# Last eight modulation rows beside the first group's quads, and a column order for the first three down products

## The chip, the cores and the metric

One core of a Trainium2 chip runs the whole program. The metric is device time in microseconds. Before the change three runs gave 2177.98, 2178.56 and 2180.01 us, median 2178.56 us.

## The reference

One decoder layer over 2048 tokens of width 1024, in float32. The modulation vector `mod` has 6 x 1024 values; its last 1024, `gate2`, scale only the result of the feed-forward part.

```python
def reference(x, c, positions, w_ada, b_ada, ...):
    mod = silu(c) @ w_ada + b_ada
    shift1, scale1, gate1, shift2, scale2, gate2 = split(mod, 6)
    h = modulate(rmsnorm(x, norm1_w), shift1, scale1)
    x = x + gate1 * hybrid_mixer(h, ...)      # attention heads and SSD heads
    h = modulate(rmsnorm(x, norm2_w), shift2, scale2)
    x = x + gate2 * swiglu(h, w_gate_up, w_down)   # (silu(g) * u) @ w_down
    return rmsnorm(x, final_norm_w)
```

## The kernel before

**Tiling.** Tokens are cut into four blocks of 512. A value is kept as [128 channels, 512 tokens]. Each float32 product is made of three fast matmuls: an operand is split into a rounded part (ScalarE, a copy) and a rest (VectorE, a subtraction), and hi x hi, hi x lo and lo x hi are added in one bank of PSUM. There are four rotating banks `d` (`dense()`) and four side banks.

**Stages.** First the input projections, attention and SSD of the blocks; then the feed-forward part in two groups of two blocks. The feed-forward products are of the Strassen kind: seven products take the place of eight. A *quad* (L1055 on, 22 per group) makes four weight tiles' worth of the gate/up part from seven products of 12 matmuls (lines 1050 to 1052), each with weights loaded into `raw` (5 buffers) and split into `w` (6 buffers). Its token operands are named b11, t1, b21, t2, t3, b22, t4. `quads` yields seven times per quad; `beside` hands every yield to `tick`, which moves side work on: attention and SSD of later blocks, and the modulation rows while `ada_rest` holds them.

**Modulation rows.** One row gives 128 values of `mod`. `ada_later` loads the row's two halves [128, 512] of `w_ada` into two buffers `aw` (L202) and reduces each against the silu row `csil` on VectorE (L208). `rest_of_ada` goes through rows 16 to 23, 32 to 39, 24 to 31 and 40 to 47, three ticks a row. Row 40 to 47 are `gate2`. They come last, while the second block's output projection and the last block's projections run.

**Down products.** `pairs.stage` makes one of seven down products per group, with 11 token tiles (index k) and four output columns c. `steps_of` cuts a product into 12 steps: a column c with a chunk of k (0 to 3, 4 to 7, 8 to 10). A step loads and splits its weight tile (L1174, L1177, L1178) and issues 12 or 9 matmuls (L1182). Columns go in pairs: c 0 and 1 through all three chunks, then c 2 and 3. After a column's last chunk `done` takes its bank: a copy into `t` for b11 (L1228); for b21 and t4 a residual block `t` is loaded (L1197), the bank is added to it (L1213) and it is stored. b11 and t4 start new banks, b21 goes on in those of b11.

The token tiles come from DRAM (`tokens_of`): a load (L1162), a ScalarE copy (L1163), a VectorE subtraction (L1164). They share 11 buffers `a`, one product's worth, so a token tile of the next product can only be loaded when the last matmul on its buffer is over. For the first three products of the first group the caller asks for four tiles after the ninth step, four after the tenth, and the last three after the twelfth. Beside them run `last_operands`, the operands of the second group (lines 914 to 932 and 1028 to 1041), on VectorE, ScalarE, GpSimd and the DMA queue.

**Order.** The program is written down in this order; a scheduler then sets each engine's order by a simulated timeline, except that PE keeps the written order up to the end of the last block's projections. `behind(engine)` keeps an instruction from going ahead of the one written just before it on that engine. Each engine works its list in order, SP's list of DMA issues too: an issue that waits holds up those behind it.

## Time and profile before

| what | value |
|---|---|
| three runs, median | 2178.56 us |
| profiled execution, its time | 2179.79 us |
| profiled execution, its span | 2177.7 us |
| mean granted TensorE clock | 0.997 |
| ACT busy, share of the span | 47% |
| POOL busy, share of the span | 25% |
| DMA moved | 466.76 MB, mean 214 GB/s |

The span is the time from the first to the last instruction of the profiled execution; 2.1 us lie around it. PE is TensorE's matmuls, PEld its weight loads, DVE is VectorE, ACT ScalarE, POOL GpSimd, SP the engine that issues the DMAs. In the rows that stand in the prediction a name such as `a<-act_t` reads "writes a, reads act_t", `L1182` is a line of the kernel, and "x12" a count.

### The profile page before, as it was taken

How to read it: one execution, taken by the hardware profiler on the slowest of the kernel's cores; microseconds unless marked ns; L12 is line 12 of the kernel's file. 1: busy time of each engine (PE TensorE's matmuls, PEld its weight loads, DVE VectorE, ACT ScalarE, POOL GpSimd, SP SyncE). 2: the span in 40 equal slices, each digit the busy share in tenths (PEclk: the TensorE clock that was granted, in tenths of full speed). 3: DMA queues.
4: the chain of work that ended last, by engine and by line, in shares of the span. 5: the costliest groups of instructions: out<-in, count | busy, mean ns of one | idle time of the engine just before them, and what ended most of it. 6: DMA issues, size and time to landing. Idle time of an engine off the chain costs nothing.

```text
span 2177.7 us, 33314 instructions
## 1 busy us (share of the span) xinstructions
PE 2139.7 (98%) x10984; PEld 1764.9 (81%) x10984; DVE 1651.1 (76%) x3195; ACT 1016.5 (47%) x2137; POOL 553.5 (25%) x658
## 2 busy tenths in 40 slices
PE   8989999999999999999999999999999999999998
PEld 6889898879778777788888878788888888888887
DVE  6987857885778866798897678777877765886576
ACT  3675735653557454433344445433333334554441
POOL 0223433322112211243441212333333331210011
PEclk9999999999999999999999999999999999999999
DMA  7798978797998332333335778645555536778553
GB/s 269 237 341 297 353 260 312 255 342 238 360 357 313 109 97 92 121 109 124 115 94 178 248 244 293 216 155 187 166 167 179 168 112 232 239 266 278 184 161 105
DMA packets 287708, 466.76 MB, mean 214 GB/s; under 512 B 27440, under 2 KB 97072, under 8 KB 287536
## 3 DMA queue, kind: packets, MB, share of 16 engines
q1 hardware_dynamic: 286960, 464.13, 63.3%
q8 instruction: 86, 1.41, 0.3%
q14 instruction: 86, 0.70, 0.1%
q10 hardware_dynamic: 576, 0.52, 0.1%
HBM read 329.73 MB, written 134.81 MB: 213 GB/s over the span
## 4 chain that ended last, share of the span: by engine, by line
PE 79%; DVE 8%; DMA 5%; ACT 3%; issue 2%; POOL 1%; SPq 0%; DVEq 0%; ACTq 0%; POOLq 0%
PE d L1182 17%; PE d L1052 9%; PE d L1051 9%; PE d L1050 9%; PE d L286 4%; PE d L287 4%; PE d L288 4%; DMA aw<-in_wada_dram 1%; PE d L1323 1%; PE am L1050 1%; PE am L1052 1%; PE am L1051 1%; PE am L706 1%; PE sm L1052 1%; PE sm L1051 1%
## 5 line engine op out<-in xcount | busy, mean ns | idle before, releaser
L1182 PE MATMUL d<-a,w 128*128 128x512 f32 x1716 | 403.5, 396 | 2.2 <-DVE a L1164 2.2
L1182 PEld LDWEIGHTS d<-a,w 128*128 128x128 f32 x1716 | 323.2, 189 | 79.6 <-DVE a L1164 2.9
L1052 PE MATMUL d<-b,w 128*128 128x512 f32 x924 | 366.9, 399 | 0.6 <-DVE w L898 0.6
L1051 PE MATMUL d<-b,w 128*128 128x512 f32 x924 | 366.6, 397 | 0.7 <-DVE b L932 0.5
L1050 PE MATMUL d<-b,w 128*128 128x512 f32 x924 | 363.2, 397 | 0.0
L897 ACT ACTIVATE w<-s 128x512 fp32r<-128x512 f32 x176 | 111.0, 631 | 237.2 <-PE d L1052 148.2
L1051 PEld LDWEIGHTS d<-b,w 128*128 128x128 f32 x924 | 174.2, 189 | 41.7 <-DVE b L932 1.5
L1052 PEld LDWEIGHTS d<-b,w 128*128 128x128 f32 x924 | 173.8, 188 | 40.4 <-DVE w L898 1.0
L1050 PEld LDWEIGHTS d<-b,w 128*128 128x128 f32 x924 | 174.2, 189 | 38.0
L286 PE MATMUL d<-w,hl 128*128 128x256 f32 (+1 forms) x592 | 171.9, 290 | 2.7 <-DVE s L511 2.7
L287 PE MATMUL d<-w,hl 128*128 128x256 f32 (+1 forms) x592 | 166.9, 282 | 0.0
L288 PE MATMUL d<-w,hl 128*128 128x256 f32 (+1 forms) x592 | 166.8, 282 | 0.0
L1178 DVE TENSOR_TENSOR w<-raw,w 128x512 fp32r<-128x512 f32 x156 | 114.0, 739 | 43.3 <-ACT w L1177 43.0
L1104 POOL TENSOR_TENSOR t<-t 128x512 f32<-128x512 f32 x44 | 75.5, 1717 | 277.0 <-DVE t L1103 126.1
L1164 DVE TENSOR_TENSOR a<-a 128x512 fp32r<-128x512 f32 x154 | 106.2, 704 | 46.1 <-ACT a L1163 45.3
L898 DVE TENSOR_TENSOR w<-s,w 128x512 fp32r<-128x512 f32 x176 | 131.1, 746 | 6.3 <-ACT w L897 5.4
L1163 ACT ACTIVATE a<-a 128x512 fp32r<-128x512 f32 x154 | 96.1, 629 | 85.1 <-DMA a<-act_t 50.1
L296 POOL TENSOR_TENSOR acc<-acc,t 128x512 f32<-128x512 f32 x35 | 51.8, 1481 | 325.7 <-ACT t L295 312.1
L286 PE MATMUL d<-hl,w 128*128 128x512 f32 x320 | 131.6, 411 | 0.0
L288 PE MATMUL d<-hl,w 128*128 128x512 f32 x320 | 126.1, 394 | 0.0
L1177 ACT ACTIVATE w<-raw 128x512 fp32r<-128x512 f32 x156 | 90.6, 587 | 75.8 <-PE d L1182 44.3
L287 PE MATMUL d<-hl,w 128*128 128x512 f32 x320 | 125.7, 393 | 0.0
(426 smaller groups left out, 4802.6 us busy)
## 6 DMA issues: line engine op xcount, KB each, us to landing
raw<-in_wgu_dram SPq DMA_DIRECT2D x176, 256.0 KB, 3.0
act_t<-t SPq DMA_DIRECT2D x88, 256.0 KB, 2.9
a<-act_t SPq DMA_DIRECT2D x88, 256.0 KB, 4.5
act_b<-t SPq DMA_DIRECT2D x66, 256.0 KB, 2.0
a<-act_b SPq DMA_DIRECT2D x66, 256.0 KB, 4.2
aw<-in_wada_dram SPq DMA_DIRECT2D x64, 256.0 KB, 5.1
w<-w_x SPq DMA_DIRECT2D x32, 512.0 KB, 5.5
raw<-wd_s SPq DMA_DIRECT2D x64, 256.0 KB, 3.2
```

Source lines behind the costliest of these rows:

```text
L286: nc.tensor.matmul(out, ahi, bhi, start=first, stop=False)
L287: nc.tensor.matmul(out, ahi, blo, start=False, stop=False)
L288: mm3.last = nc.tensor.matmul(out, alo, bhi, start=False, stop=last)
L897: nc.scalar.activation(hi, x, AF.Copy)
L898: eng.tensor_tensor(lo, x, hi.bitcast(F32), ALU.subtract)
L1050: nc.tensor.matmul(out, ahi, bhi, start=first and k == 0, stop=False, skip_group_check=True)
L1051: nc.tensor.matmul(out, ahi, blo, start=False, stop=False, skip_group_check=True)
L1052: mm3.last = nc.tensor.matmul(out, alo, bhi, start=False, stop=k == 3, skip_group_check=True)
L1163: nc.scalar.activation(hi, raw, AF.Copy)
L1164: nc.vector.tensor_tensor(lo, raw, hi.bitcast(F32), ALU.subtract)
L1178: nc.vector.tensor_tensor(w[1], raw, w[0].bitcast(F32), ALU.subtract)
L1182: mm3.last = nc.tensor.matmul(ps, w[x][:, ws], act[k][y], start=new and k == 0 and x + y == 0, stop=k == KP - 1 and x == 1, skip_group_che ...
```

## The change

Two edits. The first takes rows 40 to 47 out of `rest_of_ada`, stores the silu row in DRAM (`csil_d`), and makes the eight rows later, beside the first group's quads, from step 12 on: first the left halves of all eight rows, then the right halves, each through the one buffer `acc` of `sums()`, with half of the silu row at a time in a small pool that takes the place of a pool closed by then. The second gives `steps_of` a column order for the first three products: all four columns of a chunk of k before the next chunk, and a call for one token tile of the next product after each step from the fifth on.

```diff
-    def steps_of(act, src, banks, new, done):
-        for c, (lo, hi) in ((c + e, chunk) for c in (0, 2) for chunk in CHUNKS for e in range(2)):
+    def steps_of(act, src, banks, new, done, across):
+        order = [(c + e, chunk) for c in (0, 2) for chunk in CHUNKS for e in range(2)]
+        if across:
+            order = [(c, chunk) for chunk in CHUNKS for c in range(4)]
+        for c, (lo, hi) in order:
...
-            return steps_of(act, of, self.banks, name not in ("b21", "b22"), done)
+            return steps_of(act, of, self.banks, name not in ("b21", "b22"), done, not self.pool)
...
     def rest_of_ada():
-        for i in (*range(16, 24), *range(32, 40), *range(24, 32), *range(40, 48)):
+        for i in (*range(16, 24), *range(32, 40), *range(24, 32)):
             yield from ada_later(i)
...
+        with behind(mybir.EngineType.SP):
+            nc.sync.dma_start(csil_d, csil)
+    def gates_of_ada(pool):
+        parts = small([P, 8], "part", 1, pool=pool)
+        for half in range(2):
+            hs = slice(half * T, (half + 1) * T)
+            c = big("cs", 1, pool=pool)
+            with behind(mybir.EngineType.SP):
+                nc.sync.dma_start(c, csil_d[:, hs])
+            for j in range(8):
+                i = 40 + j
+                with behind(mybir.EngineType.SP):
+                    w = sums()
+                    nc.sync.dma_start(w, wada[i, :, hs])
+                for _ in range(2):
+                    yield
+                src, dst = (parts[:, j:j + 1], mod[:, i:i + 1]) if half else (b_ada[:, i:i + 1], parts[:, j:j + 1])
+                with behind(mybir.EngineType.DVE):
+                    nc.vector.tensor_tensor_reduce(w, w, c, 0.5, src, ALU.mult, ALU.add, dst)
+                yield
         nc.vector.tensor_scalar(gate2, gate2, 0.5, None, ALU.mult)
...
-    for _ in beside(main, lambda i: RATIO_UP if i >= 6 else 0):
+    ada_rest.clear()
+    gating = ExitStack()
+    rest = gates_of_ada(gating.enter_context(tc.tile_pool(name="gates", bufs=1, side="right")))
+    for i in beside(main, lambda i: RATIO_UP if i >= 6 else 0):
+        if i == 12:
+            ada_rest.append(rest)
         if not sides:
             break
     finish(sides[-1] if sides else None)
+    drain(rest)
+    ada_rest.clear()
+    gating.close()
...
-                if after and i in (8, 9):
-                    for _ in range(4):
-                        next(coming, None)
+                if after and i > 3:
+                    next(coming, None)
```

Where the change moves instructions, first PE at the start of the third product, t4. `d_...` is a column's bank, `a_...` a token tile, `w_...` a weight tile. Before, 14787 to 14799 are k 0 to 3, 14820 on k 4 and up, and 14902, 14920, 15014 are columns 0, 1, 2:

```order
L1182 MATMUL d_14902<-a_14799,w_14905 128x512 x2
L1182 MATMUL d_14920<-a_14787,w_14923 128x512 x2
L1182 MATMUL d_14920<-a_14791,w_14923 128x512 x3
L1182 MATMUL d_14920<-a_14795,w_14923 128x512 x3
L1182 MATMUL d_14920<-a_14799,w_14923 128x512 x3
L1182 MATMUL d_14902<-a_14820,w_14946 128x512
L1182 MATMUL d_14920<-a_14820,w_14963 128x512
L1182 MATMUL d_14902<-a_14820,w_14946 128x512 x2
L1182 MATMUL d_14902<-a_14824,w_14946 128x512
L1182 MATMUL d_14920<-a_14820,w_14963 128x512 x2
```

The same place now (k 0 to 3 are 14714 to 14777, k 4 is 14805; columns 14905, 14923, 14947, 14965):

```order
L1185 MATMUL d_14923<-a_14756,w_14926 128x512 x3
L1185 MATMUL d_14923<-a_14777,w_14926 128x512 x3
L1185 MATMUL d_14905<-a_14805,w_14985 128x512
L1185 MATMUL d_14947<-a_14714,w_14950 128x512 x3
L1185 MATMUL d_14947<-a_14735,w_14950 128x512 x3
L1185 MATMUL d_14947<-a_14756,w_14950 128x512 x3
L1185 MATMUL d_14947<-a_14777,w_14950 128x512 x3
L1185 MATMUL d_14965<-a_14714,w_14968 128x512 x3
L1185 MATMUL d_14965<-a_14735,w_14968 128x512 x3
L1185 MATMUL d_14965<-a_14756,w_14968 128x512 x3
L1185 MATMUL d_14965<-a_14777,w_14968 128x512 x3
L1185 MATMUL d_14905<-a_14805,w_14985 128x512 x2
```

Before, k 4 was wanted after 24 matmuls of the product; now 24 more on k 0 to 3 stand ahead of it, but for one hi x hi matmul of k 4, which stands where it was.

Second, DVE where the second product ends and the third begins. L1164 makes the rest of a token tile of t4, L1213 takes a bank of b21, L1178 is a weight tile, the others are second-group operands. Before, from the third bank of b21:

```order
L1036 TENSOR_TENSOR t<-t 128x512
L1213 SCALAR_TENSOR_TENSOR t<-d,mod,t 128x512
L932 TENSOR_TENSOR b<-t,b 128x512
L1178 TENSOR_TENSOR w<-raw,w 128x384
L1039 SCALAR_TENSOR_TENSOR t<-t,mod 128x512
L1213 SCALAR_TENSOR_TENSOR t<-d,mod,t 128x512
L1164 TENSOR_TENSOR a<-a 128x512
L1178 TENSOR_TENSOR w<-raw,w 128x384
L1164 TENSOR_TENSOR a<-a 128x512
```

The same place now, where L1178 is called L1181 and L1213 is L1216; the first L1164 rows are k 0 to 3 of t4, and the L1216 is the first bank of b21:

```order
L1164 TENSOR_TENSOR a<-a 128x512 x2
L1041 SCALAR_TENSOR_TENSOR t<-t,mod 128x512
L1181 TENSOR_TENSOR w<-raw,w 128x384
L1164 TENSOR_TENSOR a<-a 128x512
L932 TENSOR_TENSOR b<-t,b 128x512
L1164 TENSOR_TENSOR a<-a 128x512
L1181 TENSOR_TENSOR w<-raw,w 128x512
L921 SCALAR_TENSOR_TENSOR t<-t,scl_146,at 128x512
L1181 TENSOR_TENSOR w<-raw,w 128x512
L927 SCALAR_TENSOR_TENSOR b<-t,mod,b 128x512
L1216 SCALAR_TENSOR_TENSOR t<-d,mod,t 128x512
L1164 TENSOR_TENSOR a<-a 128x512
```

So k 0 to 3 now stand ahead of all four banks of b21, and k 4 (the last row) behind the first bank; before, k 4 stood behind the fourth.

Third, SP in the first group's quads. L903 loads quad weights, L1098 stores quad results, L1499 loads half of the silu row and L1504 half a modulation row into `acc`. Now:

```order
L1098 DMA act_t_219<-t 128x512
L1499 DMA cs<-csil_d 128x512
L1504 DMA acc<-in_wada_dram 128x512
L903 DMA raw<-in_wgu_dram 128x512
L1504 DMA acc<-in_wada_dram 128x512
L903 DMA raw<-in_wgu_dram 128x512
L1504 DMA acc<-in_wada_dram 128x512
L1098 DMA act_b_213<-t 128x512
```

The rows of L1499 and L1504 are new there, among the loads and stores of the quads. Each L1504 after the first waits until DVE has reduced the half row before it, since `acc` is one buffer; the weight loads and stores behind it wait too.

More of the change, by code (lines that the diff above doesn't have):

```diff
@@ L1484, in rest_of_ada @@
                 nc.vector.tensor_tensor(dsh, sh2[:, 4:8], sh2[:, 0:4], ALU.subtract)
+        with behind(mybir.EngineType.SP):
+            nc.sync.dma_start(csil_d, csil)
+    csil_d = dr.tile([P, D], F32, name="csil_d")
+    def gates_of_ada(pool):
[16 more added lines that the diff above has]
+                yield
         nc.vector.tensor_scalar(gate2, gate2, 0.5, None, ALU.mult)
```

## The prediction

> **What bounds the kernel now.** First the busy shares of the page, then its costliest group:
>
> ```profile
> PE 2139.7 (98%) x10984; PEld 1764.9 (81%) x10984; DVE 1651.1 (76%) x3195; ACT 1016.5 (47%) x2137; POOL 553.5 (25%) x658
> L1182 PE MATMUL d<-a,w 128*128 128x512 f32 x1716 | 403.5, 396 | 2.2 <-DVE a L1164 2.2
> ```
>
> PE is the bound. The down products (L1182) wait once, 2.2 us, for a token tile that VectorE splits. No edit here takes a matmul away, so all that can be won is time in which PE stands or runs slowly. The windows show how much there is of it. Columns: stretch, its length, then busy time (and instructions) of PE, PEld, DVE, ACT, POOL, then the granted clock, the DMA engines' share, GB/s:
>
> ```profile
> 100.00:150.00 50.00, 43.47 (x291) 38.21 (x289) 47.33 (x119) 41.27 (x96) 14.79 (x16) 1.00 0.93 329
> 574.00:645.00 71.00, 70.67 (x357) 55.11 (x356) 48.65 (x128) 36.27 (x88) 5.97 (x9) 1.00 0.98 343
> 686.00:716.00 30.00, 27.62 (x137) 20.83 (x137) 24.95 (x42) 22.12 (x49) 10.28 (x8) 0.94 0.69 246
> 735.00:910.00 175.00, 175.00 (x858) 136.31 (x857) 123.93 (x250) 89.77 (x216) 26.75 (x21) 1.00 0.32 100
> 1350.00:1400.00 50.00, 47.84 (x200) 38.20 (x199) 39.40 (x61) 27.13 (x48) 15.14 (x7) 0.97 0.82 284
> 1650.00:1700.00 50.00, 50.00 (x217) 40.59 (x217) 38.25 (x56) 17.03 (x30) 14.50 (x10) 1.00 0.60 193
> ```
>
> From 1650 to 1700 us PE does nothing but matmuls of 512 columns, 217 in 50 us, one per 0.230 us: full speed. From 1350 to 1400 us it does the same kind and gets through 200. The missing 17 are 17 x 0.230 = 3.9 us. The quads from 735 to 910 us lose nothing. In the first feed-forward steps, 686 to 716 us, PE is idle 2.4 us and the clock is below 1. The two low clocks, closer:
>
> ```profile
> 686.00:689.45 3.45, 2.48 (x18) 2.10 (x17) 2.09 (x8) 1.76 (x4) 1.04 (x1) 1.00 1.05 377
> 689.45:692.86 3.41, 3.30 (x10) 2.84 (x11) 1.94 (x8) 2.76 (x11) 0.00 (x0) 0.50 1.01 362
> 1364.90:1367.40 2.50, 0.36 (x2) 0.00 (x0) 2.50 (x4) 1.99 (x5) 0.65 (x1) 1.00 1.05 397
> 1368.70:1372.10 3.40, 3.40 (x10) 2.63 (x9) 3.40 (x7) 1.67 (x3) 2.27 (x1) 0.50 0.62 224
> ```
>
> Twice a wait of PE is followed by 3.4 us at half clock, in which half the work gets done: 1.7 us lost each time. So the loss around 1365 us is a wait of 2.15 us (row below) and 1.7 us of half clock, together 3.9 us: the same as the matmuls that are missing. That is the price of one late tile.
>
> **The second edit: the column order.** PE, then DVE, where the third product t4 begins:
>
> ```profile
> 1367.42 26.38 PE L1182 MATMUL d<-a,w 128*128 128x512 f32 x106 [2.15 <-DVE a L1164]
> ...
> 1362.59 0.74 DVE L1213 SCALAR_TENSOR_TENSOR t<-d,mod,t 128x512 f32<-128x512 f32 x1
> 1363.26 0.68 DVE L932 TENSOR_TENSOR b<-t,b 128x512 fp32r<-128x512 f32 x1
> 1363.86 0.55 DVE L1178 TENSOR_TENSOR w<-raw,w 128x384 fp32r<-128x384 f32 x1
> 1364.32 1.78 DVE L1039 SCALAR_TENSOR_TENSOR t<-t,mod 128x512 f32<-128x512 f32 x1
> 1366.03 0.74 DVE L1213 SCALAR_TENSOR_TENSOR t<-d,mod,t 128x512 f32<-128x512 f32 x1
> 1366.69 0.67 DVE L1164 TENSOR_TENSOR a<-a 128x512 fp32r<-128x512 f32 x1
> ```
>
> PE resumes when the L1164 of 1366.69 us ends: k 4, the fifth tile of t4. 106 matmuls follow of the product's 132, so 26 were done: the two steps on k 0 to 3 and a first pair on k 4. k 4 was late for two reasons. Its buffer came free only after the eighth step of b21, and it was wanted 24 x 0.230 = 5.5 us into t4. The edit moves both. Four columns now use k 0 to 3 before k 4 is touched, so k 4 is wanted 48 x 0.230 = 11.0 us into the product, 5.5 us later; and each chunk's buffers come free as soon as its four steps are done, so k 0 to 3 can be loaded after the fourth step instead of the eighth, four steps of 12 or 9 matmuls (9.7 us) sooner. In DVE's new list k 4 stands behind the first bank of b21 instead of the fourth. One hi x hi matmul of k 4 still stands after 24; it needs ScalarE's half alone. The slack is some 5.5 + 9 us against a lateness of 2.15 us, so I take the whole loss as gone: **A = 3.9 us**. Nothing is added: the same steps, loads and splits.
>
> What is late next? The banks. Now all four columns end in the last four steps, and t4 opens on the first one's bank: between the end of column 0 and the first matmul of t4 lie three steps of 9 matmuls, 27 x 0.230 = 6.2 us. In that time the residual block must have landed and L1213 run.
>
> ```profile
> L1197 SPq DMA_DIRECT2D t<-mid x8: 320/354/534, 1339.7 to 1366.5; - x8
> ...
> DMA to landing us min/median/max: 3.0/4.2/5.9
> ...
> 1328.52 0.58 ACT L1228 ACTIVATE t<-d 128x512 f32<-128x512 f32 x1
> ```
>
> The first two rows are the eight residual loads and their times from issue to landing. They are issued ahead of the bank's end where a `t` buffer is free, so the usual lag is L1213's 0.74 us behind what DVE has in hand (0.5 to 1.8 us above); a load issued only when the column ends would take 5.9 + 0.74 = 6.6 us, 0.4 us too long. I take 0, with 0.4 us plus a half clock of 1.7 us, 2.1 us, as the far end. b21's opening needs only the copy L1228, 0.58 us of ScalarE.
>
> **The first edit: the eight rows.** What it takes away, by the reduction's two forms and the loads (KB each, median us to landing):
>
> ```profile
> L208 DVE CUSTOM_DVE_ANT_0 aw<-aw,csil,vec x32: 737/746/919, 271.7 to 652.7; 128x512 f32<-128x512 f32 x32
> L208 DVE CUSTOM_DVE_ANT_0 aw<-aw,csil,part x32: 722/751/1666, 272.8 to 654.7; 128x512 f32<-128x512 f32 x32
> ...
> aw<-in_wada_dram SPq DMA_DIRECT2D x64, 256.0 KB, 5.1
> ```
>
> 16 reductions of 0.75 us, 12.0 us of DVE, and 16 loads of 256 KB, 4.2 MB; at the 343 GB/s of the window from 574 to 645 us, where they stood, 12.2 us of all DMA engines. That window runs at 0.98 of the DMA engines, and yet PE is idle for 0.33 us in it: there is nothing to win inside. What can be won is behind it, where operands and weights that queued behind these loads and reductions are wanted. The waits of PE and PEld from 686 to 716 us (total, times, longest):
>
> ```profile
> PE am L697 <- DVE ast L672: 1.1, 1, 1.1
> PE d L1052 <- DVE w L898: 0.6, 1, 0.6
> PE d L1051 <- DVE b L932: 0.5, 1, 0.5
> ...
> PEld d L1051 <- DVE b L932: 1.5, 3, 0.8
> PEld d L1052 <- DVE w L898: 1.0, 1, 1.0
> ```
>
> L932 (the operands b22, t3, t2, t4) and L898 (quad weights) are DVE work that a shorter DVE list brings forward; as the weight loads see it they cost 1.5 + 1.0 = 2.5 us. L697 waits for attention scores that PE itself has just made; only what stands between them could hide it. All of it with one half clock of 1.7 us is 1.1 + 2.5 + 1.7 = 5.3 us at most. The same reshuffle can place another wait there, of the size of those now seen: down to -1.1 us. I take half of the DVE waits, 1.2 us, and half of the half clock, 0.8 us: **B = 2.0 us**, since the lists move by a dozen microseconds but each short chain keeps its own length.
>
> What it adds, between 735 and 910 us or so: 48 yields after the twelfth, seven a quad, hence seven quads. 16 reductions of 0.75 us, 12 us, fit into DVE's 175 - 123.9 = 51 us of idle time; 18 loads fit into DMA engines at 0.32. The store of the silu row (512 KB) adds 0.5 MB to a window that loses 4.2 MB. The waits go to SP's list: a row's load waits for the reduction before it, and quad weights queue behind. What covers that:
>
> ```profile
> ACT w L897 <- PE d L1052: 188.0, 105, 4.8
> SPq L1098 <- POOL t L1110: 27.1, 4, 10.0
> ```
>
> ScalarE waits 105 times for PE to give back a `w` buffer, so the split weights run as far ahead as the six buffers allow: 6 x 12 x 0.230 = 16.6 us of PE's work. SP already stands up to 10.0 us behind one store with no wait on PE. A reduction is 0.75 us and its load some 5; I take **C = 0**, with 0.6 us, one wait as L1052's above, as its dear end.
>
> **The sum**, against the profiled execution's own 2179.79 us: 3.9 + 2.0 + 0 = 5.9 us less, 2173.9 us. That execution lies 1.2 us above the median of the three runs, 2178.56 us; from the median it is **2172.6 us**, 0.27% less.
>
> **The rivals.**
> *The wait moves to the banks or stays* (A = 0 to 1.8): DMA engines at 1.05 around 1365 us and an SP list in order speak for it, the 6.2 us of slack against it. 2178.56 - 2.0 - 0.9 = 2175.7 us.
> *The first edit brings nothing* (B = 0): the waits at 686 to 716 us hang on chains of attention. 2178.56 - 3.9 = 2174.7 us.
> *Half clocks are no matter of these waits* and come anyway. For it: PE waited 2.7 us once between 100 and 150 us, and the clock there stayed at 1.00:
>
> ```profile
> PE d L286 <- DVE s L511: 2.7, 1, 2.7
> ```
>
> Against it: the only two low clocks inside the kernel follow a wait by 1 to 2 us. Then A is 2.15 and B 1.2 us, 2175.2 us. The Trainium skill, "TensorE: Matmul & The Clock Gate", section "What's actually happening", speaks for this rival: the clock falls to half after an idle window of about 3.4 us, and neither wait is that long. The trace disagrees, with half clock after waits of 2.15 and 1.1 us, so I follow the trace.
> *Slower: SP is held by the rows in the quads.* If SP stands longer than the 16.6 us of split weights, PE waits in every such row. From 0.65 us a row on, 16 x 0.65 = 10.4 us outweigh 5.9 us by over 0.2% (4.4 us): 2183 us. SP's longest stand of 10.0 us speaks against it.
> *It does not do what it says*: a `t` or `a` buffer held elsewhere keeps the token tiles as late as now. That is the first rival's time.
>
> **How the numbers follow.** 0.2% is 4.4 us, about what a measurement can tell from no change. Forecast 0.53; wait moves or stays 0.15; first edit nothing 0.13; half clocks anyway 0.13; slower 0.06. Low end: A, most of B and the three runs' lowest, 2177.98 - 3.9 - 4.1 = 2170.0. High end: the first rival with C's 0.6 and the highest of the three runs, 2177.7. Below 2174.2 us counts as faster: nearly all of the forecast's own share and a fifth of the middle rivals', 0.59; within 0.2%, 0.35; slower 0.06.
>
> **What would show it.** In the new trace: 217 matmuls in 50 us through the first three down products and clock 1.00 there; no wait of L1182's line on DVE a; L1213's new line early enough that no wait on DVE t shows on PE. From 686 to 716 us fewer waits on L932 and L898, and perhaps no half clock. From 735 to 910 us PE at 175.00 of 175.00. Wrong would be a wait of L1182 at the opening of b21, t4 or the second group's first quad, or PE idle in the quads with SP waiting for the reductions.

## The result and the profile after

The changed kernel took 2184.71 us (median of 7 runs) against 2177.98 us (median of 7) before: ratio 1.0035, 95% interval 1.0026 to 1.0045. It was forecast 5.9 us faster and is 6.7 us slower. The busy shares and two of the costliest groups of the page of the changed kernel (L1185 is L1182 of before):

```profile
PE 2144.2 (98%) x10984; PEld 1767.0 (81%) x10984; DVE 1649.9 (76%) x3195; ACT 1013.3 (46%) x2137; POOL 552.6 (25%) x658
...
L1185 PE MATMUL d<-a,w 128*128 128x512 f32 x1716 | 401.9, 395 | 0.1
L1050 PE MATMUL d<-b,w 128*128 128x512 f32 x924 | 365.7, 400 | 3.3 <-ACT a L1163 3.0 <-ACT b L931 0.3
```

The down products no longer wait for a token tile: the 2.2 us of L1182 are 0.1 us now. But the quads' L1050 has a new wait of 3.0 us, and for a token tile too. The windows, with the columns of those before:

```profile
686.00:716.00 30.00, 25.71 (x124) 17.87 (x121) 23.93 (x41) 20.39 (x47) 10.05 (x8) 0.94 0.61 209
735.00:910.00 175.00, 175.00 (x861) 136.03 (x861) 135.15 (x283) 89.04 (x216) 27.94 (x20) 1.00 0.39 123
1350.00:1400.00 50.00, 46.87 (x200) 37.29 (x199) 41.99 (x61) 26.45 (x49) 12.15 (x7) 0.99 0.80 266
1395.10:1398.55 3.45, 0.43 (x3) 0.04 (x1) 2.71 (x5) 3.37 (x7) 1.34 (x1) 1.00 0.56 213
1399.23:1402.64 3.41, 3.41 (x10) 2.62 (x9) 3.41 (x7) 0.74 (x2) 0.00 (x0) 0.50 0.73 250
```

From 1350 to 1400 us PE gets through the same 200 matmuls as before: the loss that the second edit was to remove has moved some 30 us down the program, half clock included. From 686 to 716 us PE is idle 4.3 us instead of 2.4. Its waits there (total, times, longest):

```profile
PE d L1051 <- DVE b L927: 3.2, 2, 2.2
PE am L697 <- DVE ast L672: 0.6, 1, 0.6
```

To compare kernels that differ in order, I cut the program at instructions that all have. The *quads stretch* runs from the last projection matmul to the first output projection matmul, both of line L286. Before, then after:

```profile
L286 PE MATMUL d<-w,hl x64: 278/282/387, 651.6 to 677.9; 128*128 128x256 f32 x64
...
L286 PE MATMUL am<-mo,w x32: 391/396/400, 1195.3 to 1242.3; 128*128 128x512 f32 x32
```

```profile
L286 PE MATMUL d<-w,hl x64: 278/282/388, 651.9 to 678.2; 128*128 128x256 f32 x64
...
L286 PE MATMUL am<-mo,w x32: 391/395/400, 1200.8 to 1247.8; 128*128 128x512 f32 x32
```

It takes 517.3 us before and 522.6 after. The *down stretch*, from the first down product to the end of the last matmul, takes 876.8 us before and 878.2 after. These two, +5.3 and +1.4 us, make up 6.7 of the 6.8 us between the spans (2177.7 and 2184.5). The stretches repeat better than whole times: in the six profiles in which the rows stay where they were and nothing is added beside the quads, the quads stretch is 517.24 to 517.33 us, and one kernel profiled twice (e9 and e17 below) has down stretches of 873.3 and 874.0 us, while the whole runs of one kernel spread over 2 to 11 us.

### The profile page after: what moved, and what is told of

Read it like the earlier page. It is cut to its first block, busy times and chain, and to the rows that moved or that the text cites. A ratio compares the mean times of both kernels' runs of the same rounds, so it can differ in the third digit from the quotient of the medians.

```text
span 2184.5 us, 33312 instructions
## 1 busy us (share of the span) xinstructions
PE 2144.2 (98%) x10984; PEld 1767.0 (81%) x10984; DVE 1649.9 (76%) x3195; ACT 1013.3 (46%) x2137; POOL 552.6 (25%) x658
## 4 chain that ended last, share of the span: by engine, by line
PE 85%; DVE 6%; DMA 4%; issue 2%; ACT 2%; SPq 1%; POOL 0%; DVEq 0%; ACTq 0%; POOLq 0%
PE d L1185 16%; PE d L1052 10%; PE d L1051 10%; PE d L1050 10%; PE d L286 6%; PE d L288 5%; PE d L287 5%; PE d L1326 1%; PE am L1050 1%; PE am L1052 1%; PE am L1051 1%; PE am L706 1%; PE sm L818 1%; PE sm L1052 1%; PE sm L1051 1%
## 5 line engine op out<-in xcount | busy, mean ns | idle before, releaser
L1185 PE MATMUL d<-a,w 128*128 128x512 f32 x1716 | 401.9, 395 | 0.1
L1185 PEld LDWEIGHTS d<-a,w 128*128 128x128 f32 x1716 | 322.1, 188 | 77.0 <-issue 2.4
L1051 PE MATMUL d<-b,w 128*128 128x512 f32 x924 | 368.8, 399 | 3.2 <-DVE b L927 3.2
L1050 PE MATMUL d<-b,w 128*128 128x512 f32 x924 | 365.7, 400 | 3.3 <-ACT a L1163 3.0
L1052 PE MATMUL d<-b,w 128*128 128x512 f32 x924 | 367.4, 398 | 0.0
L897 ACT ACTIVATE w<-s 128x512 fp32r<-128x512 f32 x176 | 110.7, 630 | 234.1 <-PE d L1052 142.3
L1051 PEld LDWEIGHTS d<-b,w 128*128 128x128 f32 x924 | 175.1, 190 | 44.4 <-DVE b L927 4.6
L1050 PEld LDWEIGHTS d<-b,w 128*128 128x128 f32 x924 | 174.6, 189 | 42.7 <-ACT a L1163 3.4
L1052 PEld LDWEIGHTS d<-b,w 128*128 128x128 f32 x924 | 174.5, 189 | 39.7 <-DVE t L1103 0.4
L286 PE MATMUL d<-w,hl 128*128 128x256 f32 (+1 forms) x592 | 172.6, 292 | 2.7 <-DVE s L511 2.7
L1164 DVE TENSOR_TENSOR a<-a 128x512 fp32r<-128x512 f32 x154 | 107.5, 711 | 55.9 <-ACT a L1163 55.4
L1181 DVE TENSOR_TENSOR w<-raw,w 128x512 fp32r<-128x512 f32 (+1 forms) x156 | 116.2, 753 | 39.8 <-ACT w L1180 39.4
L1163 ACT ACTIVATE a<-a 128x512 fp32r<-128x512 f32 x154 | 96.1, 628 | 102.1 <-DMA a<-act_t 65.0
L286 PE MATMUL d<-hl,w 128*128 128x512 f32 x320 | 131.6, 411 | 0.4 <-DVE stp L565 0.4
L1180 ACT ACTIVATE w<-raw 128x512 fp32r<-128x512 f32 (+1 forms) x156 | 90.2, 586 | 66.0 <-PE d L1185 44.5
```

Source lines behind the costliest of these rows:

```text
L286: nc.tensor.matmul(out, ahi, bhi, start=first, stop=False)
L897: nc.scalar.activation(hi, x, AF.Copy)
L1050: nc.tensor.matmul(out, ahi, bhi, start=first and k == 0, stop=False, skip_group_check=True)
L1051: nc.tensor.matmul(out, ahi, blo, start=False, stop=False, skip_group_check=True)
L1052: mm3.last = nc.tensor.matmul(out, alo, bhi, start=False, stop=k == 3, skip_group_check=True)
L1163: nc.scalar.activation(hi, raw, AF.Copy)
```

## The experiments

All runs, with the ratio to the kernel before and the two stretches of the profiled execution. "Low" is where half clock began inside the two stretches; it lasts one window of 3.4 us each time, but two in e16 and e18 near 706 us. Of each edit below only the lines that matter are shown; `...` and the text stand for the rest.

| run | ratio, 95% interval | quads | down | low at us |
|---|---|---|---|---|
| before | | 517.3 | 876.8 | 689, 1369 |
| changed kernel | 1.0035, 1.0026 to 1.0045 | 522.6 | 878.2 | 706, 959, 1399 |
| e1_rows_only | 1.0026, 1.0016 to 1.0036 | 522.0 | 875.3 | 704 |
| e2_order_only | 1.0011, 1.0002 to 1.0019 | 517.2 | 876.0 | 687 |
| e3_order_held | 0.9997, 0.9987 to 1.0008 | 517.3 | 874.0 | |
| e5_after_held | 1.0024, 1.0015 to 1.0033 | 522.2 | 874.2 | 709 |
| e6_removed | 1.0019, 1.0010 to 1.0028 | 520.0 | 875.0 | 707 |
| e7_added | 1.0033, 1.0020 to 1.0045 | 520.6 | 877.7 | 692, 954, 1371 |
| e8_sums_held | 1.0023, 1.0013 to 1.0033 | 520.3 | 876.5 | 706 |
| e4_calls_only | 1.0004, 0.9995 to 1.0013 | 517.3 | 874.4 | 689 |
| e9_order_old_calls | 0.9993, 0.9984 to 1.0002 | 517.3 | 873.3 | 686 |
| e10_both_held | 1.0014, 1.0005 to 1.0024 | 520.3 | 873.6 | 701 |
| e11_no_loads | 1.0026, 1.0011 to 1.0040 | 520.0 | 875.3 | 702 |
| e13_loads_kept | 1.0014, 1.0004 to 1.0024 | 520.3 | 876.8 | 698, 1371 |
| e16_rows_later | 1.0075, 1.0059 to 1.0091 | 531.8 | 875.7 | 706 |
| e17_order_old_calls_again | 0.9992, 0.9983 to 1.0001 | 517.2 | 874.0 | 687 |
| e18_later_apart | 1.0061, 1.0044 to 1.0078 | 526.8 | 874.5 | 705, 961 |
| e19_rows_apart | 1.0056, 1.0041 to 1.0071 | 527.8 | 874.3 | 710 |

### Each edit alone

**e1_rows_only**: the second edit is undone.

```diff
-                if after and i > 3:
-                    next(coming, None)
+                if after and i in (8, 9):
+                    for _ in range(4):
+                        next(coming, None)
```

> Kernel: the first edit alone; the down products keep their old order of columns and their old calls for token tiles. Theory (T): most of the 6.7 us comes from the rows. Taking them out of VectorE's list before 686 us reorders that list, and the rest of operand b22 (L927) now stands behind sums of quad weights (L1059): the waits and half clock at 700 to 750 us cost 2.3 us more than before, and a half clock at 959 us that before did not have costs 2.4 us more. So 4.7 us above the kernel before, ratio 1.0022 (1.0012 to 1.0030), with waits of PE L1051 on DVE b L927 of 1 to 2 us and two half clocks at 706 and 959 us. Rival (R): the rows are harmless and all of the loss is the second edit's: ratio 0.9990 to 1.0003, no wait on L927.

**e2_order_only**: the first edit is undone.

```diff
-        for i in (*range(16, 24), *range(32, 40), *range(24, 32)):
+        for i in (*range(16, 24), *range(32, 40), *range(24, 32), *range(40, 48)):
```

> Kernel: the second edit alone; the rows stay where they were. Theory (T): the wait of t4 on its fifth token tile (2.15 us and a half clock of 1.7 us) goes, and the first quad of the second group waits 3.0 us instead, with a half clock of 1.7 us, because ScalarE, in order, has a copy of a token tile of t2 ahead of that quad's weight splits and that tile's load has not landed. Net 0.8 to 1.3 us above the kernel before: ratio 1.0005 (0.9998 to 1.0011), PE L1050 waits on ACT a L1163 near 1397 us. Rival (R): the second edit carries the whole loss of 6.7 us: ratio 1.0030. Second rival (S): the wait at the first quad comes only together with the moved rows; then ratio 0.9982.

By their times both edits cost, and the costs add: 1.0026 and 1.0011 against 1.0035. The first edit is the larger, and in its profile all of its loss lies in the quads stretch (+4.7 us); the second half clock expected at 959 us did not come in it. The second edit leaves the quads stretch as it was. Its loss of 0.11% is shown by the times alone: in its one profile the down stretch is 0.8 us shorter than before. The expected wait of 3.0 us on L1163 did not come either; the first quad waits twice, 1.1 us for a bank that L1216 gives back and 1.2 us for a copy (L1074), without half clock.

### The second edit: who makes the first quad wait

ScalarE of the changed kernel between the last down product and the first quad of the second group, then SyncE's queue, then PE:

```profile
1395.18 0.63 ACT L1163 ACTIVATE a<-a 128x512 fp32r<-128x512 f32 x1 [6.80 <-DMA a<-act_t]
1395.71 0.61 ACT L897 ACTIVATE w<-s 128x512 fp32r<-128x512 f32 x1
1396.23 0.61 ACT L1163 ACTIVATE a<-a 128x512 fp32r<-128x512 f32 x1
1396.75 0.61 ACT L897 ACTIVATE w<-raw 128x512 fp32r<-128x512 f32 x1
```

```profile
1381.96 8.98 SPq L903 DMA_DIRECT2D raw<-in_wgu_dram  x4
1391.03 0.86 SPq L1162 DMA_DIRECT2D a<-act_t  x2
```

```profile
1398.54 0.47 PE L1050 MATMUL d<-b,w 128*128 128x512 f32 x1 [3.02 <-ACT a L1163]
```

L1163 splits token tiles of t2. They are needed only after the 22 quads (22 x 84 matmuls x 0.230 = 425 us later), and are written near the end of the quads' loop. But their loads need nothing except free `a` buffers, so the scheduler puts them wherever buffers come free, and in the new column order that is the end of t4. ScalarE stands 6.80 us for such a tile, whose load SyncE issues only at 1391 us, behind 9 us of weight loads (L903), and the splits of the first quad's weights (L897) stand behind it. PE has nothing to multiply. ScalarE of e2_order_only stands for such a tile too, ahead of the copy that its first quad waits for:

```profile
1396.63 0.63 ACT L1163 ACTIVATE a<-a 128x512 fp32r<-128x512 f32 x1 [6.67 <-DMA a<-act_t]
1397.17 0.61 ACT L897 ACTIVATE w<-raw 128x512 fp32r<-128x512 f32 x1
1397.68 0.58 ACT L1074 ACTIVATE t<-d 128x512 f32<-128x512 f32 x1
```

**e3_order_held** is the second edit alone, **e5_after_held** the whole change, each with these loads held back. In the whole change this moves t2's tiles, and with them five weight sums and splits on VectorE and one PE product near 1806 us:

```diff
             if i >= 7 * NF - 16:
-                next(coming, None)
+                with behind(mybir.EngineType.SP):
+                    next(coming, None)
```

> Kernel: the second edit alone, and each load of a token tile of t2 is held behind the SyncE load written before it, so that it cannot be moved ahead of the second group's quads. Theory (T): both the wait in t4 and that in the first quad are gone, with their half clocks: 3.5 to 4.7 us less than the second edit alone, ratio to the kernel before 0.9982 (0.9975 to 0.9990), granted clock 1.00 from 1350 to 1450 us. Rival (R): the first quad waits for its own weights (loads issued late, or the operands of last_operands), not for the copies of t2 ahead of them; then a wait of 2 to 3 us stays there and the ratio is that of the second edit alone, near 1.0005.

> Kernel: the whole change, and t2's token loads held back as in the run with the second edit alone. Theory (T): 4.7 us less than the changed kernel, about 2180.0 us, ratio to the kernel before 1.0012 (1.0003 to 1.0020): what is left is the first edit's loss at 700 to 750 and at 959 us. Rival (R): the wait at the first quad is no matter of t2's loads; ratio stays 1.0035 (1.0026 to 1.0045).

The waits at the first quad are gone in both, and in e5 the half clock behind them; 2.0 and 4.0 us leave the down stretch. The stretch from 1350 to 1400 us in the run e3_order_held:

```profile
1350.00:1400.00 50.00, 49.74 (x215) 39.82 (x214) 38.98 (x56) 22.03 (x40) 12.59 (x7) 1.00 0.73 239
```

215 matmuls of the 217 that full speed makes: what the prediction wanted to see. The ratios fell from 1.0011 to 0.9997 and, with the rows, from 1.0035 to 1.0024. That is the forecast direction, but both lie above the forecast ratios (0.9982 and 1.0012). Those counted both waits with a half clock each, and not every execution has them: the wait in t4 is shorter in most profiles, and e2's has no half clock at the first quad.

**e4_calls_only** has the new calls with the old order of columns, **e9_order_old_calls** the new order with the old calls and t2 held; **e17_order_old_calls_again** repeats e9. The rows are in their old place in all three.

```diff
 e4_calls_only
-        if across:
-            order = [(c, chunk) for chunk in CHUNKS for c in range(4)]
 e9_order_old_calls, e17_order_old_calls_again, with t2's hold
-                if after and i > 3:
-                    next(coming, None)
+                if after and i in (8, 9):
+                    for _ in range(4):
+                        next(coming, None)
```

> Kernel: of the second edit only the calls: one token tile of the next product is asked for after each step from the fifth on, with the old order of columns; rows in their old place. Theory (T): the buffers of k 4 and later still come free only in the last four steps, so t4's fifth tile stays late: a wait of 1.3 to 2.2 us on L1164 at about 1367 us, with or without a half clock of 1.7 us behind it; the stretch from the first down product to the last matmul stays within 1.8 us of before's, ratio 0.9995 to 1.0005. Rival (R): asking earlier alone is enough; no wait of L1182, and 2 to 4 us less in that stretch.

> Kernel: of the second edit only the order of columns, with the old calls for token tiles at the ninth and tenth step; the loads of t2's token tiles held back; rows in their old place. The stretch from the first down product (L1182) to the last matmul took 876.8 us in the kernel before (with one half clock), 874.4 with the new calls alone, and 874.0 with order, calls and held loads. Theory (T): the column order alone takes t4's fifth tile out of the way, since k 4 is wanted 24 matmuls later: no wait of L1182 above 0.9 us, stretch 874.0 to 874.9 us, ratio 0.9990 to 1.0000. Rival (R): without the early calls the tiles k 0 to 3 of t4 come after the ninth step and t4 opens late: a wait of 1.5 to 3 us at its opening, stretch 875.5 to 878 us, ratio 1.0000 to 1.0010.

> Kernel: the column order alone with the old calls for token tiles and t2's token loads held back, a second time. Theory (T): it takes away the wait of t4 and the half clock that sometimes follows, and puts nothing in its place: 1 to 3.4 us less in the stretch from the first down product to the last matmul, which was 873.3 us the first time against 874.0 to 877.7 us in the other kernels; ratio 0.9993 with an interval that now ends below 1. Rival (R): the first time was a lucky set of runs; ratio 0.9997 to 1.0003.

Asking earlier alone leaves t4's fifth tile late (wait of 1.5 us); the half clock did not come, and the down stretch is 2.4 us shorter than before, where 1.8 at most was expected. The column order alone is enough: no wait of the down products in e9, 0.6 us in e17. Both intervals just reach 1, so the interval below 1 that e17 was to bring did not come. Together their 21 runs average 2174.92 us and the 46 runs of before beside them 2176.58: 1.67 us less, with 0.95 us as two standard errors. This version beats the changed kernel clearly and the one before by 0.08%.

### The first edit: removal and addition

**e6_removed** takes the rows away and makes them nowhere (`gate2` is half of its bias alone); **e7_added** keeps them and makes them again beside the quads, into a spare tile. Both have the old column order. The lines of e6 are set against the kernel before, those of e7 against the changed kernel:

```diff
 e6_removed
-        for i in (*range(16, 24), *range(32, 40), *range(24, 32), *range(40, 48)):
+        for i in (*range(16, 24), *range(32, 40), *range(24, 32)):
...
-        nc.vector.tensor_scalar(gate2, gate2, 0.5, None, ALU.mult)
+        nc.vector.tensor_scalar(gate2, b_ada[:, 40:48], 0.5, None, ALU.mult)
 e7_added
-        for i in (*range(16, 24), *range(32, 40), *range(24, 32)):
+        for i in (*range(16, 24), *range(32, 40), *range(24, 32), *range(40, 48)):
...
-                src, dst = (parts[:, j:j + 1], mod[:, i:i + 1]) if half else ...
+                src, dst = (parts[:, j:j + 1], spare[:, j:j + 1]) if half else ...
```

> Kernel: the eight rows are taken out of their old place and are made nowhere; gate2 is half of its bias alone, so the modulation's last 1024 values are left out. Column order and token tiles as before. The stretch from the last projection matmul (L286, near 678 us) to the first output projection matmul (L286, near 1195 us), in which nothing but the first group's quads and their side work runs, took 517.3 us before and 522.0 us with the rows made beside the quads. Theory (T): the loss has two halves. Taking the rows away reorders PE and VectorE around 690 to 705 us, which alone costs the waits on b22 (L927, 3 to 4 us in all); the rest, 1.5 to 2 us of waits around 955 and 985 us, comes from the rows' reductions standing in VectorE's list. So this stretch takes 519.5 to 520.5 us here and the ratio is 1.0008 to 1.0018. Rival (R): it is the added work in the quads that costs; then the stretch is back at 517.3 us or less, no wait on L927, ratio 0.9985 to 1.0000.

> Kernel: the eight rows stay in their old place, and are made a second time beside the first group's quads, into a spare tile that nothing reads. Theory (T): without the removal PE and VectorE keep something like their old order at 690 to 705 us, so no wait on b22 of more than 1 us; the stretch from the last projection matmul to the first output projection matmul takes 518 to 519.5 us, 0.7 to 2 us more than before, from waits of L818 around 955 us; ratio 1.0003 to 1.0010. Rival (R): the added reductions and loads carry the whole loss: stretch 522 us, ratio 1.0022 to 1.0030.

Taking work away costs 2.65 us of the quads stretch (517.31 to 519.96). With the rows added as well it is 522.03. So about half is the removal and the other half the addition, as expected of e6_removed. The expectation for e7_added failed: adding without removing gave 520.6 us with a wait of 2.5 us on another operation (L1050 on a copy of L1074) at 691 us and two half clocks.

Where the time goes can be read by counting the quads' matmuls (L1050 to L1052) from the last projection matmul on. By how much they start later than in the kernel before, in us:

| quad matmul, its start before | e6 | e1 | e7 | changed kernel | e8 (below) |
|---|---|---|---|---|---|
| 169th, 735 us | 2.6 | 2.8 | 0.4 | 2.2 | 0.9 |
| 925th, 949 us | 2.6 | 3.0 | 0.3 | 2.4 | 2.4 |
| 1093rd, 999 us | 2.6 | 4.8 | 3.4 | 5.4 | 2.8 |

The removal costs by 735 us all that it costs. e7's long wait at 691 us is hardly its loss, since its quads are only 0.4 us late behind it. In e1, e7 and the changed kernel the added rows cost next to nothing to 949 us and then 1.9 to 3.1 us by 999 us, though the last of their reductions is over by 919 us; in e7 and the changed kernel, which lose most there, a half clock begins at 954 and 959 us.

VectorE of the changed kernel where PE waits (at 703.13 us for 1.03, at 706.50 us for 2.17 us):

```profile
700.52 1.22 DVE L927 SCALAR_TENSOR_TENSOR b<-t,mod,b 128x512 fp32r<-128x512 f32 x1
701.67 0.15 DVE L687 TENSOR_TENSOR ast<-ast 128x4 f32<-128x4 f32 x1
701.74 0.67 DVE L1103 TENSOR_TENSOR t<-t,d 128x512 f32<-128x512 f32 x1
702.34 0.74 DVE L927 SCALAR_TENSOR_TENSOR b<-b,mod 128x512 fp32r<-128x512 f32 x1
703.00 0.17 DVE L688 RECIPROCAL ast<-ast 128x4 f32<-128x4 f32 x1
703.09 1.69 DVE L1059 TENSOR_TENSOR s<-raw 128x512 f32<-128x512 f32 x1
704.70 3.44 DVE L927 SCALAR_TENSOR_TENSOR b<-b,mod 128x512 fp32r<-128x512 f32 x2
```

L927 is the rest of operand b22. A sum for the next quad's weights (L1059) has slipped in ahead of the last two. **e8_sums_held** is the first edit with that sum held behind the third L927, **e10_both_held** the whole change with both holds:

```diff
-        nc.vector.tensor_tensor(s1, a21, a22, ALU.add)
+        with tc.issue_after(operands_kept.last.ins) if behind else nullcontext():
+            nc.vector.tensor_tensor(s1, a21, a22, ALU.add)
```

> Kernel: the first edit alone, and the second quad's first sum of weights (L1059) is held on VectorE behind the third L927, the rest of operand b22 for k 2. Theory (T): PE's wait of 2.2 us on L927 is made of that sum standing ahead on VectorE (1.68 us); held back, the wait is 0.3 to 0.7 us, most often without a half clock, and the stretch of the first group's quads is 1.5 to 2 us shorter than in the run of the first edit alone, if the rest of the order stays as good: 520 to 520.5 us, ratio 1.0010 to 1.0020. Rival (R): b22 is late for another reason (its load or ScalarE's half); wait and stretch stay at 2.2 and 522.0 us.

> Kernel: the whole change with both holds: t2's token loads behind the SyncE load written before them, and the second quad's first sum of weights behind the third L927. Theory (T): the two add up: the stretch of the first group's quads takes 520.3 us as with the second hold alone, the stretch from the first down product 874.2 us as with the first hold alone; against the changed kernel 2.3 and 4.0 us less, ratio to the kernel before 1.0010 to 1.0020. Rival (R): either hold turns the order elsewhere and its gain is lost: ratio 1.0024 or more.

The second wait falls from 2.2 to 0.7 us and the stretch to 520.3 us, as forecast, though the half clock came all the same: of the 2.8 us lost by 735 us in e1, 0.9 are left. The order turned further on as well: a wait of 1.3 us of L818 at 931 us that e1 does not have. Both holds add up, to 1.0014. The time of e8 (1.0023 against 1.0026) is too coarse to show what the stretch shows.

What of the removal turns the order? **e11_no_loads** takes away the rows' loads but keeps 16 reductions of the same size there, on the silu row; **e13_loads_kept** keeps the loads and takes the reductions away. Neither makes the rows beside the quads.

```diff
 e11_no_loads, load is i < 40
-        with behind(mybir.EngineType.SP):
-            for w, hs in zip(ws, halves):
-                nc.sync.dma_start(w, wada[i, :, hs])
+        if load:
+            with behind(mybir.EngineType.SP):
+                for w, hs in zip(ws, halves):
+                    nc.sync.dma_start(w, wada[i, :, hs])
...
-                nc.vector.tensor_tensor_reduce(w, w, csil[:, hs], 0.5, src, ALU.mult, ALU.add, dst)
+                nc.vector.tensor_tensor_reduce(w, w if load else csil[:, hs], csil[:, hs], 0.5, src, ALU.mult, ALU.add, dst)
 e13_loads_kept, reduce is i < 40, between the loads and the reductions
+        if not reduce:
+            yield
+            return
```

> Kernel: the rows' 16 loads are taken out of the old place, but VectorE still makes 16 reductions of the same size there, of the silu row with itself; no rows beside the quads. The last 1024 modulation values, gate2, are left out. PE's order is that of the kernel with the rows removed; VectorE's list has the 16 reductions as before the change. Theory (T1): what costs is PE's order, in which quads stand ahead of attention work that used to cover the operands; it is set by the loads. Then the stretch of the first group's quads stays at 519.5 to 520.5 us, with waits on L927 of 2 to 4 us in all; ratio 1.0010 to 1.0025. Theory (T2): what costs is VectorE's list; with the reductions back the stretch returns to 517.0 to 518.0 us, ratio 0.9995 to 1.0005.

> Kernel: the 16 loads of the eight rows stay in their old place, into tiles that nothing reads; their reductions are taken out and no rows are made beside the quads. The last 1024 modulation values, gate2, are left out. Theory (T1): the loads keep the operands' own loads where they were, so PE's order at 686 to 716 us is close to that before: no wait on L927 above 1 us, stretch of the first group's quads 517.0 to 518.3 us, ratio 0.9990 to 1.0005. Theory (T2): it is the lighter VectorE list that turns the order: stretch 519.5 to 521 us, waits on L927 of 2 to 4 us, ratio 1.0010 to 1.0025.

The waits of PE from 686 to 716 us, in e6_removed, in e11_no_loads (its L1052 and L928 are L1051 and L927) and from 690 us in e13_loads_kept (L1053 and L934 are L1050 and L931):

```profile
PE d L1051 <- DVE b L927: 3.7, 3, 2.2
```

```profile
PE d L1052 <- DVE b L928: 3.7, 3, 2.2
```

```profile
PE d L1053 <- ACT b L934: 3.7, 1, 3.7
```

In e11 VectorE's work is back, PE's order is that of e6_removed (the records of the two profiles differ in 4 of 10984 places, those of e9 and e17, one kernel, in 10), and the stretch is the same 520.0 us. So the cause is not how busy VectorE is. It is the order: one sum's place on VectorE made 1.7 us of e1's stretch, as e8 shows. That PE's own new order makes the rest is likely but not shown, since no run has the old order of PE without the rows. e13 answers neither theory as put: with the loads back the wait is not on L927, yet it is as long, at another operand, and the stretch is 520.3 us. Loads gone (with or without the reductions) or reductions gone: two new orders of PE at 686 to 716 us, and the stretch takes 2.65 to 2.94 us more with each than with the one that the kernel before happens to have.

### What the added rows cost

**e16_rows_later** is the first edit with the rows begun after the sixtieth yield instead of the twelfth. **e18_later_apart** is the same with four yields between load and reduction, **e19_rows_apart** has four yields at the place of the change.

```diff
 e16_rows_later, e18_later_apart
-        if i == 12:
+        if i == 60:
 e18_later_apart, e19_rows_apart
-                for _ in range(2):
+                for _ in range(4):
                     yield
```

> Kernel: the first edit alone, but the rows beside the quads begin after the sixtieth yield instead of the twelfth, so that their reductions run from about 915 to 1085 us instead of 746 to 915 us. Up to the sixtieth yield PE's order is that of the kernel with the rows removed. Theory (O, the order): the reductions cost nothing by their length; what they cost is the order that they turn further on. Then the waits of the removal stay (L927, 3.5 to 4 us in all near 700 us), the stretch of the first group's quads is between that with the rows removed, 520.0 us, and that of the first edit, 522.0 us, wherever the new order falls, and no wait of PE names a reduction or its load; ratio 1.0014 to 1.0026. Theory (W, the work): 16 reductions of 0.75 us and their loads take VectorE and SyncE from the SSD side work at 920 to 990 us, where PE waits for L740 and L738 anyway; standing right there they cost more than before that stretch: 522.5 us or more, ratio 1.0026 or more.

> Kernel: as with the rows begun after the sixtieth yield, but each row's reduction comes four yields behind its load instead of two. The same 16 loads and 16 reductions beside the same SSD side work, only that a load has more time to land before VectorE reaches its reduction. In the run with two yields VectorE stood idle 12.9 us, 5 times, for loads of the rows, with state sums (L811) and others queued behind it, and the stretch of the first group's quads took 531.8 us. Theory (L, the loads): it is VectorE's waits for these loads that cost; with four yields they fall below 3 us and the stretch to 520.5 to 524 us, ratio 1.0015 to 1.0035. Rival (W, the work): the 12 us of the reductions themselves cost, in a part of the program where VectorE is busy 148 of 170 us; the stretch stays at 528 us or more, ratio 1.0055 or more.

> Kernel: the first edit alone, begun after the twelfth yield as in the change, with four yields instead of two between a row's load and its reduction. Theory (L, the loads): VectorE's waits for these loads (13.5 us, 6 times, in the run of the first edit) go, and with them the 2 us that the rows cost beside those of the removal: stretch of the first group's quads 519.8 to 521.0 us, ratio 1.0010 to 1.0022. Rival (W, the work): the reductions now reach on into the SSD side work at 920 to 1020 us, and each of the last eight costs its 0.75 us there: stretch 524 us or more, ratio 1.0030 or more.

Where the rows stand decides: the same 16 reductions cost 2.1 us over e6_removed when they run from 746 to 915 us (e1), 11.8 us from 911 to 1072 us (e16; 1.0 us of them is lost by 735 us already, with the longer half clock at 706 us). e18, where they reach on to 1181 us, costs 6.9 us, and e19, whose second eight run from 896 to 1031 us, 7.9 us. From 915 us on PE works through the SSD side work; the window of the kernel before:

```profile
910.00:1080.00 170.00, 169.50 (x814) 140.37 (x813) 147.69 (x227) 63.76 (x137) 68.44 (x91) 1.00 0.38 119
```

VectorE is busy 148 of 170 us there, against 124 of 175 from 735 to 910 us, and PE's short SSD products hang on it by chains. VectorE and PE in e16_rows_later:

```profile
1002.10 0.75 DVE L1506 CUSTOM_DVE_ANT_0 acc<-acc,cs,part 128x512 f32<-128x512 f32 x1 [1.83 <-DMA acc<-in_wada_dram]
1002.78 0.08 DVE L1506 DVE_READ_ACCUMULATOR2_ANT mod<- 128x1 f32 x1
1002.78 0.68 DVE L811 TENSOR_TENSOR state<-state,st 128x512 f32<-128x512 f32 x1
```

```profile
1003.52 0.66 PE L764 MATMUL st<-ident,m 128*128 128x128 f32 x4 [1.71 <-DVE state L811]
```

A reduction (L1506) stands 1.83 us for its own load, in VectorE's order, ahead of the SSD state sum (L811) that PE waits 1.71 us for. A wait of 0.91 us at 967.89 us has a reduction that stands for its load ahead of it in the same way. The other long waits of PE there, up to 1.73 us, have no reduction just ahead. So how much of the 11.8 us is the rows' work and how much a turned order is not shown. The total of such stands in the changed kernel and in e18_later_apart:

```profile
DVE acc L1509 <- DMA acc<-in_wada_dram: 14.7, 6, 5.3
```

```profile
DVE acc L1506 <- DMA acc<-in_wada_dram: 5.6, 2, 3.2
```

Whether these stands or the 0.75 us of the reductions cost more stays open. With four yields e18 cut them from 12.9 to 5.6 us and the stretch by 5.0 us, with one half clock more in it, between both theories; in e19 they did not fall (14.5 us). And 13.5 us of them cost next to nothing in e1 while they last: from 735 to 949 us it loses 0.1 us.

## Why the prediction was wrong, step by step

In the two stretches the terms A, B and C, forecast as 3.9, 2.0 and 0 us won, came out as losses of 1.4 us (down stretch), 2.65 us (e6_removed) and 2.6 us (what remains of the quads stretch).

**The second edit, A = 3.9 us.** The mechanism was right: in every kernel with the new order t4 opens without the wait (0.9 us at most, in e5). Two steps failed.
- "Nothing is added: the same steps, loads and splits." The same loads, but the buffers that come free earlier go to whichever load is next in line: t2's loads took them and brought a wait of 3.0 us and a half clock to the next stage, 4.7 us for 3.9. The list of what would be wrong named "the second group's first quad", but no price was put on it.
- The size. The wait is not always 2.15 us with a half clock behind it. In the eleven profiles with the old column order it was 0.5 to 1.7 us eight times without one, and 2.0 to 2.2 us three times with one (before, e7, e13): 2.0 us on average with the half clocks. The two runs that keep only the gain measured 1.7 us.

**What is late next, the banks, 0 (far end 2.1).** Right: no bank is late at the openings of b21 and t4. One wait of 1.1 us for a bank of t4 stands at the second group's first quad, in e2 alone.

**The first edit, B = 2.0 us.** The sign was wrong. The step that failed is that the lists "move by a dozen microseconds but each short chain keeps its own length". The far end of -1.1 us, "the same reshuffle can place another wait there", was the mechanism, and "of the size of those now seen" its error: the new waits are 3.2 to 4.0 us in all where the sum L1059 is not held, and the removal alone costs 2.65 us of the stretch. The half of a half clock (0.8 us) was no gain to be had either: in e3_order_held it did not come at 689 us, and PE stood 1.5 us in L706 a little later instead, in the same 517.3 us:

```profile
PE am L706 <- ACT m L699: 1.5, 1, 1.5
```

The attention chain holds PE there, and the half clock at 689 us cost nothing against the one profile without it.

**The rows beside the quads, C = 0.** The cover that was named held: from 735 to 910 us PE is busy 175.00 of 175.00 us. What failed is that the sum ended there. That the reductions "fit into DVE's 175 - 123.9 = 51 us of idle time" says nothing of the SSD work behind 910 us, where e1, e7 and the changed kernel lose 1.9 to 3.1 us from 949 to 999 us, though the last reduction of the changed kernel ends at 918.6 us. Which instruction that the rows moved makes this loss stays open. The sum also counted 12.0 us of reductions but not that VectorE itself would stand 14.7 us for their loads, since there is one buffer `acc` and a load can only follow the reduction before it; up to 949 us that cost PE nothing.

**The rivals.** That SyncE is held by the rows named the right direction by the wrong mechanism, so its hit is luck: SyncE does stand for the reductions, up to 5.1 us at a time, but PE waits for nothing from 735 to 910 us. That half clocks are no matter of these waits was half right, as the last section says; and the one at 689.45 us began inside its wait (PE went on at 689.56 us), not 1 to 2 us behind it. The loss came from what the edits set free and from the order behind the rows, places that no rival priced.

## What to carry to other kernels

When an order frees buffers earlier, ask who is first in line for them: the loads that a scheduler may hoist are part of the change, and here ScalarE stood 6.80 us for a tile that was needed 425 us later. In this program, tuned with a list scheduler, taking a dozen microseconds of idle-time work away was not free: three kernels that only did so lost 2.65 to 2.94 us. So give a change that reorders a tight place a loss of that size at its far end, and not only half of the waits that it might remove. And read the idle time of an engine by stretches, on past the end of what is moved, with the stands of the moved work itself.

## What the hardware showed

Half clock keeps to a fixed grid. In the changed kernel it begins at 146.54, 706.32, 958.91 and 1399.23 us, 164, 74 and 129 times 3.413 us apart; before at 689.45 and 1368.70 us, 199 times. In the down products the length of the wait was enough to tell: waits of 2.0 us and more were followed by half clock (1.7 us lost), those of 1.7 us and less were not. The wait of 1.08 us near 689 us had half clock in five profiles of six with the same order there: in those a window of the grid ended inside the wait or 0.5 us behind it, and in the sixth (e3_order_held) one began 0.3 us ahead of it. So a wait has no fixed price. What counts in a window beside idle time is not shown: elsewhere windows with 1.3 to 1.7 us idle were not followed by half clock. The Trainium skill, "TensorE: Matmul & The Clock Gate", section "What's actually happening", says that the window of 3413 ns runs free of the kernel, and the trace agrees. The prediction set that section aside because of its idle window of about 3.4 us; but a window does not have to be idle throughout, since 2.1 of 3.4 us were enough before.
